# Sums of weight quarters formed one product ahead of their cast, out of place, in two alternating tiles

## The chip, the core and the metric

The kernel runs on one core of a Trainium2 chip. Five engines of the core work side by side, each through its own queue in order: PE (TensorE) multiplies matrices, DVE (VectorE) and ACT (ScalarE) do elementwise work, POOL (GpSimd) does a little of it, and SP (SyncE) issues the loads from memory. They wait for one another only by semaphores. PE appears twice in the profile, as PE (the matmuls) and PEld (the loads of the stationary operand that go ahead of each matmul).

The metric is the device time of one execution in microseconds. Less is better.

## The reference

The program is a two-layer decoder trunk over 512 tokens of width 1024. Each layer is a mixer, a layer norm, a SwiGLU feed-forward block and another layer norm. The change concerns the first half of the feed-forward block, which occurs once in each layer:

```python
D_MODEL, SEQ, DEPTH, D_FF = 1024, 512, 2, 2816

def swiglu(x, w_gate, w_up, w_down):
    return (jax.nn.silu(x @ w_gate) * (x @ w_up)) @ w_down

for layer in range(DEPTH):
    ...
    x = layer_norm(ALPHA * x + y, ln_mix_g[layer], ln_mix_b[layer])
    x = layer_norm(ALPHA * x + swiglu(x, ffn_w_gate[layer], ffn_w_up[layer], ffn_w_down[layer]),
                   ln_ffn_g[layer], ln_ffn_b[layer])
```

All inputs are float32. The kernel keeps that accuracy with three matmuls in a reduced format for each product: every operand is split into a high part `hi` (a cast) and a low part `lo` (the operand minus `hi`), and `hi*hi + hi*lo + lo*hi` is summed.

## The kernel before

**How a feed-forward block runs.** `ffn` (L356) handles the first two of the 22 blocks of 128 hidden features directly, prepares sums of the activations (`sums`, L322), hands the other twenty blocks to `sevens` (L394), and then multiplies by `w_down` in `down` (L276).

**What `sevens` computes.** It takes the twenty blocks as ten pairs. For one pair, `x @ w_gate` and `x @ w_up` together are seen as a product of 2 by 2 block matrices: the tokens in two halves by the inner dimension in two halves, times four weight quarters of 128 partitions by 1024 floats, which the code names `x`, `u`, `y` and `z` (gate upper, up upper, up lower, gate lower). Seven block products in place of eight give the result. Their weight operands, by position 0 to 6, are x, x+u, x+u+y, z, u+y, y, x+u+y+z. So four of the seven weights are sums that DVE must form: those of positions 1, 2, 4 and 6.

**The loop.** `sevens` has 70 steps, seven for each pair. Step i calls `make(i)` (L417), which readies the weight of product i, and `take(i - 4)` (L443), which multiplies with a weight made four steps before (`AHEAD = 4`). All engines follow the program's order in this loop (`manual_schedule`, L502). What each call issues:

- `make(i)` on DVE: where the position has a sum, the sum (L426); then on ACT the cast to `hi` (L98), and on DVE the subtraction that gives `lo` (L104). The cast needs the sum, the subtraction needs the cast, and the next step's sum stands behind this step's subtraction in DVE's queue. The text below writes sum 4, cast 4 and lo 4 for the three operations of position 4, and so on.
- The sums are in place. Position 1 writes x+u into a tile `t` (of tag `lng` for even pairs, `lnb` for odd ones), position 2 adds y to it, position 6 adds z to it; position 4 adds y to the raw tile of u. The two tags are those of the layer norm's scale and offset, whose tiles are not in use here; their next load is issued by `load_ln` (L220) after the loop.
- `take` for position 0 runs 24 matmuls into bank `a` and copies it on ACT to bank `d` (L466); for 1, into `b`, copied to `p5` (L470); for 2, on top of `d`, copied to `e` (L474); for 3, on top of `a`, then Silu on ACT (L478); for 4, on top of `e`, copied to `f` (L482) and added to `p5` on DVE (L483); for 5, on top of `d`, added on DVE (L487), and two multiplications for the first half of the tokens (L460); for 6, on top of `f`, then Silu (L493) and two multiplications for the other half (L460). Product 2 accumulates onto the copy in `d`, so PE cannot start it before the copy of L466 has ended; product 4 needs the copy of L474 in the same way, and product 6 that of L482. In the first products an extra matmul (L454) prepares a bank.

With a lead of four, step i makes the weight at position m while it takes the product at position m+3 (modulo 7). In the queue of ACT the copy of L466 therefore stands behind cast 4 of the next weights.

**Loads and buffers.** Each quarter is one load of 512 KB that SP issues (L409) into a ring of five `raw` tiles; SP waits until the ring's next tile is free. `loads` (L412) fixes the steps: x, u, y, z of pair p are issued at steps 7p-4, 7p-3, 7p-2 and 7p-1. The cast weights go into a ring of five pairs (`pair`, L106; `WP = 5`).

Of the kernel before, what the change touches and what calls it, by code (L numbers as in the profile page):

```python
# [10 lines left out]
F32 = mybir.dt.float32  # L11
# [3 lines left out]
ALU = mybir.AluOpType  # L15
AX = mybir.AxisListType

P = 128
S = 512
NB = S // P  # L20
D = 1024
# [24 lines left out]
def trunk(ctx, tc, a, out):  # L46
# [3 lines left out]
    tt = nc.vector.tensor_tensor  # L50
# [4 lines left out]
    big = ctx.enter_context(tc.tile_pool(name="big", bufs=1))  # L55
# [12 lines left out]
    def nm(s):  # L68
        cnt[0] += 1
        return f"{s}{cnt[0]}"  # L70
# [7 lines left out]
    def temp(tag="tmp", dt=F32):  # L78
        return tmp.tile([P, 512], dt, tag=tag, name=nm(tag))
# [4 lines left out]
    def ps():  # L84
        return psp.tile([P, 512], F32, tag="ps", name=nm("ps"))


    state = {"i": 0, "pool": 0}
# [8 lines left out]
    def split(src, hi, lo, pool=False):  # L97
        nc.scalar.copy(out=hi, in_=src)  # L98
        if pool:
            n = src.shape[1] // 2  # L100
            for c in (slice(0, n), slice(n, 2 * n)):
                nc.gpsimd.tensor_tensor(out=lo[:, c], in0=src[:, c], in1=hi[:, c].bitcast(F32), op=ALU.subtract)
            return
        tt(out=lo, in0=src, in1=hi.bitcast(F32), op=ALU.subtract)  # L104

    def pair(n=D):  # L106
        t = wp.tile([P, 2, D], F32R, tag="w", name=nm("w"))
        return t[:, 0, :n], t[:, 1, :n]
# [247 lines left out]
    def ffn(layer, last, flips):  # L356
# [28 lines left out]
        for f in range(2):  # L385
            for w, bank in first[2 * f:2 * f + 2]:
                gemm_a(bank, w, cols=slice(256, 512))
            finish(f, first[2 * f][1], first[2 * f + 1][1])
        last_sum()
        sevens(sx, hs, hidden_tile)  # L390
        gb = load_ln("ffn", layer)
        return down(hs, [1] * (KF - 5) + [5], gb, last)

    def sevens(sx, hs, hidden_tile):  # L394

        pairs = list(range(DIRECT, KF, 2))
        n = 7 * len(pairs)  # L400
        base = state["i"]
        state["i"] += 4 * len(pairs)
        raw, ws, tiles = {}, {}, {}

        def fetch_quarter(p, name, which):

            raw[p, name] = rawp.tile([P, D], F32, tag="raw", name=nm("raw"))
            i = base + 4 * p + which
            nc.sync.dma_start(out=raw[p, name], in_=a["w"][i // 2, :, (i % 2) * D:(i % 2) * D + D])  # L409


        loads = {}  # L412
        for p in range(len(pairs)):
            for at, args in ((-4, ("x", 0)), (-3, ("u", 1)), (-2, ("y", 2)), (-1, ("z", 3))):
                loads.setdefault(7 * p + at, []).append((p, *args))

        def make(i):  # L417

            p, pos = divmod(i, 7)
            if pos == 1:  # L420
                tag = ("lng", "lnb")[p % 2]
                raw[p, "t"] = big.tile([P, D], F32, tag=tag, name=nm(tag))
            src = raw[p, "xttzuyt"[pos]]
            if pos in (1, 2, 4, 6):
                first = raw[p, "xttzuyt"[0 if pos == 1 else pos]]
                tt(out=src, in0=first, in1=raw[p, {1: "u", 2: "y", 4: "y", 6: "z"}[pos]], op=ALU.add)  # L426
            hi, lo = pair()
            split(src, hi, lo)
            ws[i] = [t.rearrange("p (f k m) -> p f k m", f=2, k=4) for t in (hi, lo)]

        def quarter(k0, t0):
            return [[t[:, k0 + 2 * j:k0 + 2 * j + 2, t0:t0 + 256] for j in range(2)] for t in (xh, xl)]

        def product(bank, w, x, start=True):
            hi, lo = w
            for f in range(2):
                for k in range(4):
                    for m, (l, r) in enumerate(((hi, x[0]), (hi, x[1]), (lo, x[0]))):
                        mm(bank[:, f * 256:f * 256 + 256], lhsT=l[:, f, k, :], rhs=r[k // 2][:, k % 2, :],  # L439
                           start=(start and f == 0 and k == 0 and m == 0), stop=(k == 3 and m == 2),  # L440
                           skip_group_check=True)

        def take(i):  # L443


            p, pos = divmod(i, 7)
            g = tiles
            w = ws.pop(i)

            def primed():  # L450

                bank = ps()
                if p == 0 or (p == 1 and pos == 0):
                    mm(bank, lhsT=w[0][:, 0, 0, :], rhs=xh[:, 0, :], start=True, stop=True)  # L454
                return bank

            def half(n, gate, up):
                for f in range(2):
                    c = slice(f * 256, f * 256 + 256)
                    stt(out=g["h"][f][:, n * 256:n * 256 + 256], in0=gate[:, c], scalar=-1.0, in1=up[:, c],  # L460
                        op0=ALU.mult, op1=ALU.mult)

            if pos == 0:
                g["a"], g["d"] = ps(), primed()
                product(g["a"], w, quarter(0, 0))
                nc.scalar.copy(out=g["d"], in_=g["a"])  # L466
            elif pos == 1:
                g["b"], g["p5"] = ps(), temp("p")
                product(g["b"], w, sx["s1"])
                nc.scalar.copy(out=g["p5"], in_=g["b"])  # L470
            elif pos == 2:
                g["e"] = primed()
                product(g["d"], w, sx["s2"], start=False)
                nc.scalar.copy(out=g["e"], in_=g["d"])  # L474
            elif pos == 3:
                product(g["a"], w, quarter(4, 0), start=False)
                g["g0"] = temp()
                act(out=g["g0"], in_=g["a"], func=AF.Silu)  # L478
            elif pos == 4:
                product(g["e"], w, sx["s3"], start=False)  # L480
                g["f"], g["up1"] = primed(), temp("p")
                nc.scalar.copy(out=g["f"], in_=g["e"])  # L482
                tt(out=g["up1"], in0=g["p5"], in1=g["e"], op=ALU.add)  # L483
            elif pos == 5:
                product(g["d"], w, sx["s4"], start=False)
                up0 = temp("p")
                tt(out=up0, in0=g["p5"], in1=g["d"], op=ALU.add)  # L487
                g["h"] = [hidden_tile(pairs[p] + f) for f in range(2)]
                half(0, g["g0"], up0)
            else:  # L490
                product(g["f"], w, quarter(4, 256), start=False)
                g1 = temp()
                act(out=g1, in_=g["f"], func=AF.Silu)  # L493
                half(1, g1, g["up1"])
                hs.extend(g["h"])

        for at in sorted(loads):
            if at < 0:
                for args in loads[at]:
                    fetch_quarter(*args)  # L500
        E = mybir.EngineType
        with tc.manual_schedule(engines={E.PE, E.Activation, E.DVE, E.Pool, E.SP}):  # L502
            for i in range(n + AHEAD):
                for args in loads.get(i, ()):
                    fetch_quarter(*args)
                if i < n:
                    make(i)
                if i >= AHEAD:
                    take(i - AHEAD)
# [662 lines left out]
```

## Time and profile before

| | |
|---|---|
| median of 3 runs | 1101.81 us (1101.62 to 1101.85) |
| the profiled execution | 1101.23 us |
| its span | 1099.4 us |
| mean granted TensorE clock | 0.993 |
| PE busy, share of the span | 98% |
| DVE busy | 66% |
| ACT busy | 45% |
| first `sevens` on PE | about 200 to 409 us |
| second `sevens` on PE | about 762 to 972 us |

The span is the time from the first to the last recorded work of the profiled execution; the 1.8 us beyond it are the start and the end of the program. An engine's busy share is an average over the whole run, in which stages with different limits follow each other. Matmuls overlap in the pipeline, so PE shows as busy also where it could start its matmuls closer together; the distance between the starts of successive PEld records shows that better. In rows of the timeline the columns are start, duration, engine, line, operation, output and inputs, count, and in brackets the idle time just before and what ended it.

### The profile page before, as it was taken

To read this page: it belongs to the slowest core of one execution; us is meant where nothing else is said; L and a number is where in the kernel's file an instruction comes from. 1 tells how busy PE (TensorE), PEld (TensorE's weight loads), DVE (VectorE), ACT (ScalarE), POOL (GpSimd) and SP (SyncE) were. 2 spreads that over 40 slices of the span, in tenths; PEclk is the share of its full clock that TensorE was granted. 3 is DMA by queue.
4 is the path that set the end of the run, shared out by engine and by line. 5 is a ranking of instruction groups with operands and counts; after the bars stand their busy time and mean duration, and the time that the engine had idled before them with its cause. 6 is when DMAs were issued, how large, how long until landed. Compare 5 with 4: busy or idle time off the path is not lost.

```text
span 1099.4 us, 16995 instructions
## 1 busy us (share of the span) xinstructions
PE 1074.7 (98%) x6936; PEld 966.0 (88%) x6936; DVE 725.7 (66%) x1118; ACT 498.2 (45%) x831; POOL 77.7 (7%) x108
## 2 busy tenths in 40 slices
PE   9999999999999999999999999999999999999997
PEld 7888888899999998888978788888999999988885
DVE  5666449877777783334757885479777777753337
ACT  4544335545545562223466453354544544542221
POOL 0000013000000000000513411030000000000001
PEclk9999999999999999999999999999999999999999
DMA  9522222222323443331341030321332332452202
GB/s 339 194 71 78 77 78 77 75 80 97 131 81 97 144 158 101 96 98 56 96 154 58 1 115 1 102 71 58 106 126 78 107 124 78 124 183 96 96 1 76
DMA packets 31501, 109.38 MB, mean 99 GB/s; under 512 B 3504, under 2 KB 3648, under 8 KB 31424
## 3 DMA queue, kind: packets, MB, share of 16 engines
q1 hardware_dynamic: 31424, 108.31, 29.7%
q8 instruction: 54, 0.88, 0.3%
q14 instruction: 23, 0.19, 0.1%
HBM read 106.20 MB, written 2.10 MB: 99 GB/s over the span
## 4 chain that ended last, share of the span: by engine, by line
PE 57%; DVE 23%; ACT 11%; issue 8%; DMA 1%; POOL 0%; DVEq 0%; SPq 0%; ACTq 0%; POOLq 0%
PE ps L286 27%; PE ps L179 12%; ACT w L98 8%; PE ps L213 6%; DVE w L104 6%; PE ps L439 5%; DVE lng L426 3%; DVE lnb L426 3%; DVE raw L426 2%; DVE wk L460 1%; DVE xn L258 1%; PE ps L898 1%; DVE p L483 1%; DVE p L487 1%; ACT ps L474 1%
## 5 line engine op out<-in xcount | busy, mean ns | idle before, releaser
L286 PE MATMUL ps<-w,hx 128*128 128x512 f32 x1440 | 329.4, 390 | 0.0
L286 PEld LDWEIGHTS ps<-w,hx 128*128 128x128 f32 x1440 | 269.5, 188 | 55.5
L104 DVE TENSOR_TENSOR w<-raw,w 128x1024 fp32r<-128x1024 f32 (+1 forms) x175 | 212.2, 1217 | 74.4 <-ACT w L98 69.7
L439 PE MATMUL ps<-xh,w 128*128 128x256 f32 x1280 | 240.7, 286 | 7.4 <-ACT ps L466 7.4
L98 ACT CAST w<-raw 128x1024 fp32r<-128x1024 f32 (+2 forms) x184 | 189.1, 1036 | 110.8 <-DVE raw L426 73.0
L439 PEld LDWEIGHTS ps<-xh,w 128*128 128x128 f32 x1280 | 203.7, 193 | 11.1 <-ACT ps L466 11.1
L439 PE MATMUL ps<-xl,w 128*128 128x256 f32 x640 | 181.8, 284 | 0.0
L439 PE MATMUL ps<-hx,w 128*128 128x256 f32 x1440 | 179.6, 283 | 0.0
L439 PEld LDWEIGHTS ps<-hx,w 128*128 128x128 f32 x1440 | 176.0, 192 | 0.1
L179 PE MATMUL ps<-xh,w 128*128 128x512 f32 (+1 forms) x608 | 162.0, 350 | 1.1 <-ACT xh L98 1.1
L439 PEld LDWEIGHTS ps<-xl,w 128*128 128x128 f32 x640 | 123.5, 193 | 0.2
L179 PEld LDWEIGHTS ps<-xh,w 128*128 128x128 f32 x608 | 107.1, 190 | 16.7 <-ACT xh L98 1.9
L179 PE MATMUL ps<-xl,w 128*128 128x512 f32 (+1 forms) x304 | 105.4, 347 | 0.0
L104 DVE TENSOR_TENSOR hx<-m,hx 128x512 fp32r<-128x512 f32 x32 | 21.6, 689 | 81.0 <-ACT hx L98 80.9
L179 PEld LDWEIGHTS ps<-xl,w 128*128 128x128 f32 x304 | 58.0, 191 | 6.9 <-DVE xl L104 0.4
L252 POOL TENSOR_TENSOR rs<-ve,neghalf 128x1 f32<-128x1 f32 x16 | 10.5, 655 | 728.6 <-DVE ve L250 695.3
L213 PE MATMUL ps<-w,xh 128*128 128x512 f32 (+1 forms) x192 | 58.0, 383 | 0.0
L104 DVE TENSOR_TENSOR w<-lnb,w 128x1024 fp32r<-128x1024 f32 x30 | 36.7, 1225 | 31.2 <-ACT w L98 31.2
L98 ACT CAST w<-lnb 128x1024 fp32r<-128x1024 f32 x30 | 31.5, 1049 | 57.1 <-DVE lnb L426 57.1
L98 ACT CAST hx<-m 128x512 fp32r<-128x512 f32 x32 | 19.3, 623 | 83.3 <-PE ps L286 83.1
L104 DVE TENSOR_TENSOR w<-lng,w 128x1024 fp32r<-128x1024 f32 x30 | 36.7, 1224 | 29.1 <-ACT w L98 29.0
L98 ACT CAST w<-lng 128x1024 fp32r<-128x1024 f32 x30 | 31.4, 1048 | 51.9 <-DVE lng L426 51.8
(216 smaller groups left out, 1106.7 us busy)
## 6 DMA issues: line engine op xcount, KB each, us to landing
raw<-in_w_dram SPq DMA_DIRECT2D x182, 512.0 KB, 3.9
hx<-in_xT_dram SPq DMA_DIRECT2D x8, 256.0 KB, 6.0
xn<-in_xn_dram SPq DMA_DIRECT2D x4, 512.0 KB, 9.4
out_dram<-xn SPq DMA_DIRECT2D x8, 256.0 KB, 2.0
raw<-in_w_dram SPq DMA_DIRECT2D x4, 256.0 KB, 6.0
lng<-in_ln_mix_g_dram SPq DMA_DIRECT2D x2, 512.0 KB, 7.2
lnb<-in_ln_mix_b_dram SPq DMA_DIRECT2D x2, 512.0 KB, 7.5
lng<-in_ln_ffn_g_dram SPq DMA_DIRECT2D x2, 512.0 KB, 4.8
```

The costliest lines, as they stand in the source:

```text
L98: nc.scalar.copy(out=hi, in_=src)
L104: tt(out=lo, in0=src, in1=hi.bitcast(F32), op=ALU.subtract)
L179: mm(dst[:, cols], lhsT=l[:, k, :], rhs=r[:, k, cols], start=(k == 0 and n == 0), stop=(k == KD - 1 and n == 2))
L213: mm(banks[b][:, :n], lhsT=l[:, k, t], rhs=r[:, c], start=(k == 0 and m == 0), stop=(k == KD - 1 and m == 2))
L258: state["ln"] = stt(out=xn[:, b, hs], in0=r[h], scalar=rs, in1=be[:, hs], op0=ALU.mult, op1=ALU.add)
L286: mm(acc[b][h], lhsT=l[:, bs], rhs=r[:, h * 512:h * 512 + 512], start=(k == 0 and n == 0), stop=(k == nk - 1 and n == 2))
L426: tt(out=src, in0=first, in1=raw[p, {1: "u", 2: "y", 4: "y", 6: "z"}[pos]], op=ALU.add)
L439: mm(bank[:, f * 256:f * 256 + 256], lhsT=l[:, f, k, :], rhs=r[k // 2][:, k % 2, :], start=(start and f == 0 and k == 0 and m == 0), stop= ...
L460: stt(out=g["h"][f][:, n * 256:n * 256 + 256], in0=gate[:, c], scalar=-1.0, in1=up[:, c], op0=ALU.mult, op1=ALU.mult)
L474: nc.scalar.copy(out=g["e"], in_=g["d"])
L483: tt(out=g["up1"], in0=g["p5"], in1=g["e"], op=ALU.add)
L487: tt(out=up0, in0=g["p5"], in1=g["d"], op=ALU.add)
```

## The change

Three things change, all in `sevens`.

1. A new function `total(i)` forms the sum for product i. `make(i)` calls it for i+1, ahead of its own cast and subtraction. So on DVE the sum for the next product comes before the subtraction for this one. Positions without a sum (0, 3, 5) issue nothing there.
2. Of the four sums of a pair, those of positions 1, 2 and 6 are out of place: each takes a fresh tile, with the tags `lng` and `lnb` in turn over the whole loop (`state["sums"]`). Position 2 reads the tile of position 1 and position 6 that of position 2. Position 4 still adds y into the raw tile of u.
3. The loads of x and u are each one step earlier (steps 7p-5 and 7p-4); those of y and z stay.

```diff
+        state["sums"] = 0
...
-            for at, args in ((-4, ("x", 0)), (-3, ("u", 1)), (-2, ("y", 2)), (-1, ("z", 3))):
+            for at, args in ((-5, ("x", 0)), (-4, ("u", 1)), (-2, ("y", 2)), (-1, ("z", 3))):
                 loads.setdefault(7 * p + at, []).append((p, *args))
 
+        def total(i):
+
+            if i >= n:
+                return
+            p, pos = divmod(i, 7)
+            if pos == 4:
+                tt(out=raw[p, 4], in0=raw[p, "u"], in1=raw[p, "y"], op=ALU.add)
+            elif pos in (1, 2, 6):
+                tag = ("lng", "lnb")[state["sums"] % 2]
+                state["sums"] += 1
+                raw[p, pos] = big.tile([P, D], F32, tag=tag, name=nm(tag))
+                r, s = {1: ("x", "u"), 2: (1, "y"), 6: (2, "z")}[pos]
+                tt(out=raw[p, pos], in0=raw[p, r], in1=raw[p, s], op=ALU.add)
+
         def make(i):
 
             p, pos = divmod(i, 7)
-            if pos == 1:
-                tag = ("lng", "lnb")[p % 2]
-                raw[p, "t"] = big.tile([P, D], F32, tag=tag, name=nm(tag))
-            src = raw[p, "xttzuyt"[pos]]
-            if pos in (1, 2, 4, 6):
-                first = raw[p, "xttzuyt"[0 if pos == 1 else pos]]
-                tt(out=src, in0=first, in1=raw[p, {1: "u", 2: "y", 4: "y", 6: "z"}[pos]], op=ALU.add)
+            raw[p, 4] = raw[p, "u"]
+            total(i + 1)
             hi, lo = pair()
-            split(src, hi, lo)
+            split(raw[p, ("x", 1, 2, "z", 4, "y", 6)[pos]], hi, lo)
```

## The prediction

> **What bounds the kernel now.** I read the page's busy times first.
>
> ```profile
> span 1099.4 us, 16995 instructions
> ## 1 busy us (share of the span) xinstructions
> PE 1074.7 (98%) x6936; PEld 966.0 (88%) x6936; DVE 725.7 (66%) x1118; ACT 498.2 (45%) x831; POOL 77.7 (7%) x108
> ```
>
> PE is busy nearly all the time, so the change can gain no more than the pauses of PE that it removes. The waits of PEld, longest total first, begin with one row that lies wholly in `sevens`:
>
> ```profile
> PEld ps L439 <- ACT ps L466: 11.1, 17, 2.7
> ```
>
> Seventeen times a product waited for the copy of L466, 11.1 us in all, 2.7 us at the longest. It is always product 2, which accumulates onto that copy. The timeline of PEld shows one round of the loop:
>
> ```profile
> 291.53 0.19 PEld L439 LDWEIGHTS ps<-xh,w 128*128 128x128 f32 x1 [0.41 <-ACT ps L466]
> ...
> 308.80 2.95 PEld L439 LDWEIGHTS ps<-hx,w 128*128 128x128 f32 x24
> 312.15 0.19 PEld L439 LDWEIGHTS ps<-xh,w 128*128 128x128 f32 x1 [0.40 <-ACT ps L466]
> ```
>
> From the first load of product 2 (291.53) to that of product 1 in the next round (308.80) lie products 2, 3, 4, 5, 6, 0: 6 x 24 = 144 loads in 17.27 us, **0.1199 us each**, or 2.878 us for a product. Product 1 should end at 308.80 + 2.88 = 311.68, but product 2 starts at 312.15. So a pair takes 20.62 us (312.15 - 291.53), of which PE needs 168 x 0.1199 = 20.15; **0.47 us of each pair is lost**. Why the copy is late is seen on DVE and on ACT in the same stretch:
>
> ```profile
> 304.98 1.23 DVE L104 TENSOR_TENSOR w<-lnb,w 128x1024 fp32r<-128x1024 f32 x1 [1.11 <-ACT w L98]
> 306.12 0.68 DVE L487 TENSOR_TENSOR p<-p,ps 128x512 f32<-128x512 f32 x1
> 306.84 0.76 DVE L460 SCALAR_TENSOR_TENSOR wk<-tmp,p 128x256 f32<-128x256 f32 x2
> 307.51 1.22 DVE L104 TENSOR_TENSOR w<-raw,w 128x1024 fp32r<-128x1024 f32 x1
> 308.65 0.75 DVE L460 SCALAR_TENSOR_TENSOR wk<-tmp,p 128x256 f32<-128x256 f32 x2
> 309.32 1.22 DVE L426 TENSOR_TENSOR raw<-raw,raw 128x1024 f32<-128x1024 f32 x1
> 311.65 1.23 DVE L104 TENSOR_TENSOR w<-raw,w 128x1024 fp32r<-128x1024 f32 x1 [1.11 <-ACT w L98]
> ```
>
> ```profile
> 306.29 0.60 ACT L493 ACTIVATE tmp<-ps 128x512 f32<-128x512 f32 x1 [0.40 <-PE ps L439]
> 310.57 1.05 ACT L98 CAST w<-raw 128x1024 fp32r<-128x1024 f32 x1 [3.68 <-DVE raw L426]
> 311.52 0.58 ACT L466 COPY ps<-ps 128x512 f32<-128x512 f32 x1
> 312.04 1.04 ACT L98 CAST w<-raw 128x1024 fp32r<-128x1024 f32 x1
> ```
>
> Product 0 ended when product 1 began, at 308.80, so the copy could have started soon after; Silu at 306.29 shows the lag, since product 6 ended at 308.80 - 2.88 = 305.92: 0.37 us. Instead ACT stood idle 3.68 us for sum 4 (309.32), which on DVE waited behind lo 2, the addition, lo 3 and both pairs of multiplications. Sum, cast, copy: the product starts 0.05 us after the copy. DVE, in turn, idles 1.11 us behind each cast. The pair's period is that alternation, not the work of either engine:
>
> ```profile
> 309.00:330.00 21.00, 20.80 (x173) 20.60 (x172) 16.04 (x20) 10.22 (x13) 0.00 (x0) 1.00 0.30 101
> ```
>
> In these 21 us DVE (third number after the length) is busy 16.04 and ACT 10.22; the granted clock is 1.00.
>
> **The change, steady state.** No operation is added or removed: seven casts, seven subtractions and four sums per pair stay. Out of place costs nothing, by the rows of both forms (minimum, median, maximum in ns):
>
> ```profile
> L426 DVE TENSOR_TENSOR lnb<-lnb,raw x20: 1216/1218/1221, 220.2 to 959.3; 128x1024 f32<-128x1024 f32 x20
> L426 DVE TENSOR_TENSOR lnb<-raw,raw x10: 1217/1218/1220, 216.1 to 943.6; 128x1024 f32<-128x1024 f32 x10
> ```
>
> The new form, `lng` from `lnb` and raw, isn't in the trace; it has three tiles as the second row has, so 0 us, with at most 5 ns either way. A sum now runs beside a cast; the cast at 312.04 ran beside lo 4 and took 1.04, that at 310.57 beside an idle DVE took 1.05, so I take 0 for that too.
>
> Now the order, with times from the start of product 0, products back to back and their results seen 0.37 after their end. DVE: product 5 is seen at 6 x 2.878 + 0.37 = 17.64; addition to 18.3, multiplications to 19.0, then **sum 4 from 19.0 to 20.2**, ahead of lo 3. ACT: product 6 is seen at 20.15 + 0.37 = 20.52; Silu to 21.1; cast 4 has its sum already and runs to 22.1; the copy waits only for product 0 of the next pair, seen at 20.15 + 3.25 = 23.40, and ends at 24.0. Product 2 is due at 20.15 + 5.76 = 25.91. So the copy is 1.9 us early where it was 0.47 late, and PE runs through. What is late next? The copies of L474 and L482 have the same 1.9 us (one product of 2.88 lies between, less 0.37 and 0.58), with casts 6 and 1 done beforehand. The weights are three products ahead: lo 4 ends at 3.3, and its product starts at 11.5. So PE is late next, at 20.15 us a pair.
>
> For the whole stage I use the first and the last of these waits, 208.99 and 394.62 in layer 1, 770.77 and 957.18 in layer 2; each lies nine pairs apart:
>
> ```profile
> 206.12 0.19 PEld L454 LDWEIGHTS ps<-xh,w 128*128 128x128 f32 x1
> 208.99 0.19 PEld L439 LDWEIGHTS ps<-xh,w 128*128 128x128 f32 x1 [2.68 <-ACT ps L466]
> ...
> 770.77 0.19 PEld L439 LDWEIGHTS ps<-xh,w 128*128 128x128 f32 x1 [2.56 <-ACT ps L466]
> ```
>
> ```profile
> 394.62 14.66 PE ps L439 x120
> ...
> 781.17 0.23 PE ps L454
> ...
> 957.18 14.66 PE ps L439 x120
> ```
>
> PE needs 9 x 168 x 0.1199 = 181.33 us and two extra matmuls of L454 at 0.24, 181.8. Layer 1 took 185.63: **gain 3.8**. Layer 2 took 186.41: 4.6, if the clock is full. It was not:
>
> ```profile
> 770.70:774.50 3.80, 3.73 (x18) 3.73 (x19) 3.15 (x3) 1.85 (x4) 0.00 (x0) 0.55 0.45 135
> 774.50:778.30 3.80, 3.80 (x34) 3.80 (x33) 2.46 (x3) 2.20 (x3) 0.00 (x0) 1.00 0.78 254
> ```
>
> After the pause the granted clock was 0.55 for 3.8 us: 19 loads against 33, which is 14 to 15 loads or some 1.6 us lost (before, the alternation was the limit for the next three pairs and swallowed that). So **4.6 without and 3.0 with** that dip.
>
> **The change, start of the stage.** Each first product 2 waited 2.6 us for the same copy. DVE is busy without a break here, with the activation sums:
>
> ```profile
> 204.97 1.22 DVE L104 TENSOR_TENSOR w<-raw,w 128x1024 fp32r<-128x1024 f32 x1
> 206.11 1.22 DVE L426 TENSOR_TENSOR raw<-raw,raw 128x1024 f32<-128x1024 f32 x1
> ```
>
> Lo 3 stands before sum 4; the change swaps them, and the copy comes 1.14 us earlier. In the chain of layer 2 the order is the same:
>
> ```profile
> 765.70 2.27 DVE w L104 x2
> 767.97 1.15 DVE raw L426
> ```
>
> So **2.3 us** for both. Bounds: nothing, if the other additions move ahead too, and all of the pause, 2.87 - 0.24 = 2.6 us per layer, if sum 4 also comes before the activation work that precedes lo 3. I take the swap, as that is the one thing the new order forces.
>
> The clock: of two pauses of almost one length the one in layer 1 left the clock at 1.00, that in layer 2 did not. About 1.5 us of pause remains, so I expect no dip. The Trainium skill (TensorE: Matmul & The Clock Gate, Part 1: The HAM clock gate) has the clock halved after an idle window of about 3.4 us that runs freely; by that rule neither pause should have tripped it, and the trace shows that one of 2.6 us can, so the rule alone doesn't exclude a dip.
>
> **Loads.** The ring keeps its order x, u, y, z. The sums of positions 1 and 2 need u and y one step earlier; u is loaded a step earlier too, y isn't. SP issues y when lo 4 has freed the old u, at 3.3, and sum 2 comes up at about 11.7 behind lo 0 (cast 0 follows the copy of L474, seen 9.0). That leaves 8.4 us for a load of
>
> ```profile
> DMA to landing us min/median/max: 3.5/4.5/6.1
> ```
>
> so 0. The layer norm's scale, which SP loads into `lng`, must now wait for sum 6 of the last pair rather than for lo 6 of the one before, and four weight loads stand behind it on SP:
>
> ```profile
> 379.68 0.33 SPq L223 DMA_DIRECT2D lng<-in_ln_ffn_g_dram  x1
> 382.32 15.97 SPq L94 DMA_DIRECT2D raw<-in_w_dram  x4
> ```
>
> Sum 6 ends at about 4.5 in the last pair; the first of the four would land near 9 and is multiplied after 25.6 (20.15 and one product of `down`): 0.
>
> **Sum**: 3.8 + 4.6 + 2.3 = 10.7 us. The profiled execution becomes 1101.23 - 10.7 = 1090.5 (span 1088.7); the median of the runs lies 0.6 above that execution, so **1091.1 us**. Everything behind `sevens` shifts as it is: the chain's 120 matmuls after the last of these waits end the stage, and no wait at L286, the line of `down`, stands among PEld's.
>
> **Rivals.**
>
> - *The clock dips once as before.* The same work, 1.6 us more: **1092.7**. For it: a pause remains, and the windows move. Against: it is half as long.
> - *The start's pause goes wholly.* Another 1.5 us per layer: **1088**. For it: DVE's order outside the loop is planned anew. Against: the planner put the activation work first before.
> - *Half of the steady gain.* Another copy or the first pairs catch up late, or the start gains nothing: half of 3.8 + 3.0 is 3.4, so 1091.1 + 3.4 = **1094.5**, to about 1097 with the start. Against: 1.9 us of slack at each copy.
> - *Nothing changes.* DVE is the limit and has as much work as before: **1101.8**. For it: DVE is on the chain of waits. Against: 16.04 of 21 us. The Trainium skill (VectorE: DVE Perf Modes, Rules for kernel authors) says to lower the number of operations, since leaving out semaphores gains nothing; by that rule a reordering is worth 0, and the trace disagrees in so far as 1.11 us behind each cast is idle time on another engine.
> - *Slower: y comes late.* Sum 2 now stands ahead of lo 1, so a late y blocks DVE's whole queue. From sum 2 to the end of sum 4 DVE has 6.7 us of work (two sums and two subtractions at 1.14 between starts, two additions and the multiplications at 0.7), and sum 4 must end by 25.91 - 0.58 - 1.0 = 24.3 for product 2 to be on time, so y may land until 17.6, 14.3 us after its issue. From about 15 us on, the change loses (0.6 us in each of 18 pairs eats the gain of 10.7); at 16 us it costs 1.7 a pair, 31 us: 1091.1 + 31 = **1122**. Against: the longest landing is 6.1.
>
> **Chances.** Forecast 0.64, dip 0.16, whole pause 0.05, half 0.05, nothing 0.06, slower 0.04. The range, 1088.0 to 1097.0, takes in the first four and with them the bounds of the start. Faster by over 0.2% (2.2 us, about what a measurement of this kernel can tell from no change): 0.90; within: 0.06; slower: 0.04.
>
> **What would show it.** Right: the waits of PEld for L466 fall from 17 to at most two, at the starts; successive first loads of product 2 stand 20.15 apart; ACT no longer idles for L426 but for PE before L466, L470 and L474; DVE's busy time stays within 1 us of 725.7. Wrong: a wait of PE for L474 or L482, ACT's casts waiting for L426 as before, DVE waiting for a load at L426, or a first wait of 2 us or more with the clock below 1.

## The result and the profile after

The changed kernel takes **1091.57 us** (median of 4 runs, 1090.80 to 1094.18), the kernel before 1101.83 in the same comparison: a ratio of **0.9912, 95% interval 0.9897 to 0.9926**, that is 10 us less. The prediction was 1091.1. The profiled execution is the longest of the four, 1094.18 us, 2.6 us above the median; where it lost time is shown below.

The page's first rows for the changed kernel:

```profile
span 1092.4 us, 16994 instructions
## 1 busy us (share of the span) xinstructions
PE 1071.6 (98%) x6936; PEld 966.6 (88%) x6936; DVE 729.3 (67%) x1118; ACT 498.1 (46%) x831; POOL 78.6 (7%) x108
```

The work is the same; PE's share was 98% before and is 98% now, so that share would have told nothing. The waits of PEld do. Longest total first, they now begin with:

```profile
PEld ps L179 <- DVE xl L271: 5.4, 2, 2.7
```

The 17 waits for the copy into bank `d` (L466 before, L476 now) are gone, all of them, also the two at the starts. In their place stand two waits that were not there before, 2.7 us each, in another part of the feed-forward block. The chain of waits, in order of time (start, length, what), has one long row in each stage:

```profile
223.41 181.43 PE ps L449 x1512
...
783.37 181.43 PE ps L449 x1512
```

Nine pairs are one unbroken piece of 1512 matmuls in 181.43 us, 0.1200 each: before, the chain through the same stretch ran over DVE and ACT. What the stages gained is read from the starts of matmuls on PE: the first of the first product 2 (L449), and the first of `down` (L286).

```profile
208.38 0.28 PE L449 MATMUL ps<-xh,w 128*128 128x256 f32 x1
404.69 0.86 PE L286 MATMUL ps<-w,hx 128*128 128x512 f32 x3
...
768.34 0.28 PE L449 MATMUL ps<-xh,w 128*128 128x256 f32 x1
964.64 0.63 PE L286 MATMUL ps<-w,hx 128*128 128x512 f32 x2
```

In the kernel before, the first products 2 start at 208.99 and 770.77, and `down` at:

```profile
409.12 0.63 PE L286 MATMUL ps<-w,hx 128*128 128x512 f32 x2
...
971.68 0.63 PE L286 MATMUL ps<-w,hx 128*128 128x512 f32 x2
```

So the first stage takes 404.69 - 208.38 = 196.31 us from there, and the second 964.64 - 768.34 = 196.30. Before these were 409.12 - 208.99 = 200.13 and 971.68 - 770.77 = 200.91. The steady part gave **3.8 and 4.6 us**.

One round of the loop on ACT, in the timeline of the changed kernel, with L503 the Silu of product 6 and L476 the copy:

```profile
304.15 0.60 ACT L503 ACTIVATE tmp<-ps 128x512 f32<-128x512 f32 x1 [1.89 <-PE ps L449]
304.64 1.04 ACT L98 CAST w<-raw 128x1024 fp32r<-128x1024 f32 x1
306.97 0.57 ACT L476 COPY ps<-ps 128x512 f32<-128x512 f32 x1 [1.29 <-PE ps L449]
307.45 1.05 ACT L98 CAST w<-raw 128x1024 fp32r<-128x1024 f32 x1
```

and PEld at product 1 of two successive pairs:

```profile
306.65 2.95 PEld L449 LDWEIGHTS ps<-hx,w 128*128 128x128 f32 x24
...
326.81 2.95 PEld L449 LDWEIGHTS ps<-hx,w 128*128 128x128 f32 x24
```

Cast 4 (304.64) follows the Silu without a wait, where it had waited 3.68 us for its sum. ACT idles for PE now, 1.29 us before the copy. The copy ends at 307.54; product 2 is due one product after 306.65, at 309.53. It is early by 2.0 us. A pair takes 326.81 - 306.65 = 20.16 us.

### The profile page after: what moved, and what is told of

Read it like the earlier page. It is cut to its first block, busy times and chain, and to the rows that moved or that the text cites. A ratio compares the mean times of both kernels' runs of the same rounds, so it can differ in the third digit from the quotient of the medians.

```text
span 1092.4 us, 16994 instructions
## 1 busy us (share of the span) xinstructions
PE 1071.6 (98%) x6936; PEld 966.6 (88%) x6936; DVE 729.3 (67%) x1118; ACT 498.1 (46%) x831; POOL 78.6 (7%) x108
## 4 chain that ended last, share of the span: by engine, by line
PE 89%; DVE 7%; issue 1%; ACT 1%; DMA 1%; POOL 0%; DVEq 0%; SPq 0%; ACTq 0%; POOLq 0%
PE ps L449 37%; PE ps L286 27%; PE ps L179 13%; PE ps L213 5%; DVE xn L258 1%; DVE w L104 1%; DVE p L255 1%; PE ps L755 1%; DVE p L234 1%; DVE xl L271 1%; PE ps L908 1%; PE ps L604 1%; PE ps L551 1%; PE ps L591 1%; DVE st L237 1%
## 5 line engine op out<-in xcount | busy, mean ns | idle before, releaser
L286 PE MATMUL ps<-w,hx 128*128 128x512 f32 x1440 | 329.4, 390 | 0.0
L286 PEld LDWEIGHTS ps<-w,hx 128*128 128x128 f32 x1440 | 269.5, 188 | 55.5
L104 DVE TENSOR_TENSOR w<-raw,w 128x1024 fp32r<-128x1024 f32 (+1 forms) x175 | 212.2, 1217 | 65.6 <-ACT w L98 59.7
L449 PE MATMUL ps<-xh,w 128*128 128x256 f32 x1280 | 237.5, 283 | 0.0
L449 PEld LDWEIGHTS ps<-xh,w 128*128 128x128 f32 x1280 | 202.7, 192 | 0.0
L449 PE MATMUL ps<-xl,w 128*128 128x256 f32 x640 | 181.1, 283 | 0.0
L449 PE MATMUL ps<-hx,w 128*128 128x256 f32 x1440 | 179.6, 283 | 0.0
L449 PEld LDWEIGHTS ps<-hx,w 128*128 128x128 f32 x1440 | 175.9, 192 | 0.1
L179 PE MATMUL ps<-xh,w 128*128 128x512 f32 (+1 forms) x608 | 163.5, 353 | 1.4 <-ACT xh L98 1.4
L179 PEld LDWEIGHTS ps<-xh,w 128*128 128x128 f32 x608 | 108.2, 193 | 17.0 <-ACT xh L98 2.0
L449 PEld LDWEIGHTS ps<-xl,w 128*128 128x128 f32 x640 | 122.8, 192 | 0.3
L179 PE MATMUL ps<-xl,w 128*128 128x512 f32 (+1 forms) x304 | 106.3, 350 | 5.2 <-DVE xl L271 5.0
L104 DVE TENSOR_TENSOR hx<-m,hx 128x512 fp32r<-128x512 f32 x32 | 21.6, 689 | 81.0 <-ACT hx L98 81.0
L179 PEld LDWEIGHTS ps<-xl,w 128*128 128x128 f32 x304 | 58.7, 193 | 12.6 <-DVE xl L271 5.4
L104 DVE TENSOR_TENSOR hx<-wk,hx 128x512 fp32r<-128x512 f32 x28 | 19.3, 690 | 51.8 <-ACT hx L98 51.8
L104 DVE TENSOR_TENSOR w<-lnb,w 128x1024 fp32r<-128x1024 f32 x30 | 36.8, 1225 | 21.1 <-ACT w L98 21.1
L104 DVE TENSOR_TENSOR w<-lng,w 128x1024 fp32r<-128x1024 f32 x30 | 36.8, 1225 | 20.4 <-ACT w L98 20.3
L98 ACT CAST hx<-wk 128x512 fp32r<-128x512 f32 x28 | 17.4, 622 | 64.0 <-PE ps L286 61.4
```

What stands on the lines that cost most here:

```text
L179: mm(dst[:, cols], lhsT=l[:, k, :], rhs=r[:, k, cols], start=(k == 0 and n == 0), stop=(k == KD - 1 and n == 2))
L286: mm(acc[b][h], lhsT=l[:, bs], rhs=r[:, h * 512:h * 512 + 512], start=(k == 0 and n == 0), stop=(k == nk - 1 and n == 2))
```

## The new pause at the start

Why do the two waits at L179 exist? Below is DVE in the timeline of the changed kernel. L430 at 186.50 is sum 1, L104 is lo 0, L430 at 188.77 is sum 2, and L271 makes the low part of the last block's activations, which the matmuls of L179 need:

```profile
185.30 1.28 DVE L271 TENSOR_TENSOR xl<-ps,xh 128x512 fp32r<-128x512 f32 x2
186.50 1.22 DVE L430 TENSOR_TENSOR lng<-raw,raw 128x1024 f32<-128x1024 f32 x1
187.63 1.22 DVE L104 TENSOR_TENSOR w<-raw,w 128x1024 fp32r<-128x1024 f32 x1
188.77 1.22 DVE L430 TENSOR_TENSOR lnb<-lng,raw 128x1024 f32<-128x1024 f32 x1
189.90 1.28 DVE L271 TENSOR_TENSOR xl<-ps,xh 128x512 fp32r<-128x512 f32 x2
```

and PEld behind it:

```profile
190.64 0.19 PEld L179 LDWEIGHTS ps<-xl,w 128*128 128x128 f32 x1 [2.71 <-DVE xl L271]
```

In the kernel before, only sum 1 stood there:

```profile
186.67 1.21 DVE L426 TENSOR_TENSOR lng<-raw,raw 128x1024 f32<-128x1024 f32 x1
187.80 0.68 DVE L271 TENSOR_TENSOR xl<-ps,xh 128x512 fp32r<-128x512 f32 x1
```

Outside the loop the planner decides where the loop's operations fall among the others. It put sum 1, lo 0 and sum 2 in a row ahead of the subtraction. In return lo 0 and the two subtractions of the third block (L271) left the middle of the layer norm's last block, which ends sooner by that, and a pause of PE ahead of that block's flips (the transposes of L266) is gone. It stood there before:

```profile
186.15 0.42 PEld L266 LDWEIGHTS ps<-pack,xn 128*128 128x128 f32 x4 [1.25 <-issue]
```

And sum 4 came out ahead of most of the activation sums, so that the copy waits for PE only:

```profile
205.47 0.57 ACT L476 COPY ps<-ps 128x512 f32<-128x512 f32 x1 [0.46 <-PE ps L449]
```

In each stage, two pauses (about 1.3 and 2.6 us) were traded for one of 2.7. From the flips of the layer norm's third block to product 2, by matmul starts on PE, layer 1 takes 29.08 us (179.30 to 208.38), before 30.28 (178.71 to 208.99): 1.2 us gained. In layer 2 it is 30.41 (737.93 to 768.34) against 30.15 (740.62 to 770.77), 0.3 us lost. There the clock fell behind the pause; the chain has 95 matmuls behind each of the two:

```profile
190.64 11.67 PE ps L179 x95
...
749.27 13.00 PE ps L179 x95
```

```profile
749.20:752.00 2.80, 2.73 (x13) 2.73 (x14) 2.06 (x5) 1.96 (x4) 0.00 (x0) 0.50 0.35 140
```

The granted clock was 0.50 in 2.8 us, and 1.3 us went there. The terms of this execution add up to 3.82 + 4.61 + 1.20 - 0.26 = 9.37 us. Of these 2.33 were lost outside the stages: 0.59 before the flips of the first, where the granted clock was 0.83 between 5 and 15 us (1.00 before), and 1.74 in the second mixer (404.69 to 737.93 is 333.24 us, before 409.12 to 740.62, 331.50), where it was 0.50 from 650 to 655. That leaves 7.04 us, and the two profiled executions differ by 7.05. Another profiled execution of the same kernel, among the experiments, took 1090.73 us: its two stages are as long (452.23 us together from the flips to `down`, here 452.10), and the difference lies ahead of the first (1.5 us) and in the second mixer (2.1 us).

## The experiments

Two theories were tried first. **A, the cycle:** a pair's period before was a closed round of DVE and ACT taking turns, 20.62 us long, and shortening it anywhere by more than 0.47 us frees PE. **B, the one wait:** only sum 4 counts, since only its copy made PE wait. The first four kernels ran together, then the next four, and the last three side by side.

**Sum 4 alone ahead**, on the kernel before:

```diff
-            if pos in (1, 2, 4, 6):
+            if pos in (1, 2, 6):
                 first = raw[p, "xttzuyt"[0 if pos == 1 else pos]]
                 tt(out=src, in0=first, in1=raw[p, {1: "u", 2: "y", 4: "y", 6: "z"}[pos]], op=ALU.add)
+            if pos == 3:
+                d, s = {4: ("u", "y"), 6: ("t", "z")}[4]
+                tt(out=raw[p, d], in0=raw[p, d], in1=raw[p, s], op=ALU.add)
```

> The kernel before with one edit: sum 4 alone is formed one step early, ahead of lo 3, still in place; the other sums, the tiles and the loads as before. Theory A (the period of 20.62 us is a cycle of DVE and ACT taking turns, and shortening it anywhere by more than 0.47 us makes PE the limit) and theory B (only the wait of the copy at L466 for sum 4 counts) both expect the whole steady gain, 8.4 us, a pair at 20.15 us and no wait for that copy after the start. Sums 1 and 2 are not ahead, so the pause of 2.7 us before L179 that the changed kernel has should be absent, and the pause before the first product 2 should be 1.1 us shorter than before in each layer. Time 1091 us, about that of the changed kernel. Rival C (all four sums must be ahead): above 1097.

Measured: 1089.83 us, ratio 0.9900 (0.9884 to 0.9917). PEld's longest wait, with L469 the copy:

```profile
PEld ps L442 <- ACT ps L469: 3.0, 2, 1.5
```

Two waits, both at the starts and 1.1 us shorter than those of before (1.55 and 1.42 against 2.68 and 2.56), no wait at L179 for the subtraction, and in both stages 1512 matmuls in 181.43 us again, 20.16 us a pair: as expected on each point. One sum moved by one step gives what the whole change gives, or a little more.

**Sum 6 alone ahead**, the same edit with 6 for 4 and `pos == 5` for `pos == 3`:

> The kernel before with one edit: sum 6 alone is formed one step early, ahead of lo 5, still in place; sum 4 stays in its old place in front of the copy at L466. Theory A (a cycle): any one sum taken out of the cycle shortens it by 1.1 us, more than the 0.47 that are missing, so a pair still takes 20.15 us and PE waits for the copy only at the start, 2.7 us as before: 1093.5 us. Theory B (one wait): sum 4 stands where it stood, a pair keeps 20.6 us and PE waits at least 14 times: 1101 us or more.

Measured: 1094.03 us, 0.9939 (0.9924 to 0.9954).

```profile
PEld ps L442 <- ACT ps L469: 5.2, 2, 2.7
```

PE waits for the copy at the two starts only. Yet sum 4 stands where it stood, directly ahead of the cast that holds up the copy, as one round of the loop shows (cast 4 and the copy on ACT, product 1 on PEld):

```profile
308.19 1.05 ACT L98 CAST w<-raw 128x1024 fp32r<-128x1024 f32 x1 [2.77 <-DVE raw L426]
309.14 0.58 ACT L469 COPY ps<-ps 128x512 f32<-128x512 f32 x1
```

```profile
307.32 2.95 PEld L442 LDWEIGHTS ps<-hx,w 128*128 128x128 f32 x24
...
327.48 2.95 PEld L442 LDWEIGHTS ps<-hx,w 128*128 128x128 f32 x24
```

Cast 4 still waits 2.77 us for its sum. But the copy ends at 309.72, and product 2 is due at 307.32 + 2.88 = 310.20: it is 0.5 us early where it was 0.47 late, and a pair takes 20.16 us. **Theory B falls.** The copy was late because the whole round was 0.47 us too long; it was enough to cut it at sum 6, far from the wait.

**All but sum 4 ahead**, on the changed kernel:

```diff
-            total(i + 1)
+            if pos == 4:
+                total(i)
+            if pos != 3:
+                total(i + 1)
```

> The changed kernel with sum 4 put back behind lo 3 and in front of its own cast; sums 1, 2 and 6 stay ahead. Theory A: a pair takes 20.15 us, since three sums are out of the cycle. Theory B: about 20.6 us and waits of PE for the copy again. At the start the pause of 2.7 us before L179 stays, as sums 1 and 2 are ahead, and a pause of about 1.2 us before the first product 2 comes back: 1094 us by theory A, 1102 by theory B.

Measured: 1095.57 us, 0.9951 (0.9934 to 0.9967); profiled execution 1098.06.

```profile
PEld ps L179 <- DVE xl L271: 5.4, 2, 2.7
PEld ps L452 <- ACT ps L479: 2.9, 2, 1.7
```

Theory A again: nothing in the pairs (181.43 us for nine), and both kinds of pause at the starts, 2.7 and 1.3 to 1.7 us. The time lies 1.6 us above the 1094 expected; in the profiled execution the clock fell behind both pauses of 2.7 us.

**No sum ahead**, on the changed kernel (`total(i)` for `total(i + 1)`), which leaves the alternating tiles and the earlier loads:

> The changed kernel with each sum in its old place, in front of its own cast; what is left of the change are the alternating tiles out of place and the loads of x and u one step earlier. If those two cost and bring nothing, as the prediction has it: 1101.8 us within 1.5, a pair at 20.62 us, 17 waits for the copy, 11 us in all. If the earlier loads or the tiles bring part of the gain: below 1099.

Measured: 1100.93 us, 1.0001 (0.9990 to 1.0012).

```profile
PEld ps L449 <- ACT ps L476: 11.2, 17, 2.7
```

The same 17 waits as before: with the sums in their old places, those two parts cost nothing and bring nothing. By the code, the fresh tiles are what allows sum 2 to go ahead of lo 1, since in place it would overwrite x+u before lo 1 has read it. Sum 4 alone, or sum 6 alone, needs none.

**One more sum in the kernel before**, in the cycle:

```diff
                 tt(out=src, in0=first, in1=raw[p, {1: "u", 2: "y", 4: "y", 6: "z"}[pos]], op=ALU.add)
+                if pos == 1 and p:
+                    tt(out=src, in0=first, in1=raw[p, "u"], op=ALU.add)
```

> The kernel before with sum 1 formed twice in a row from the second pair on (the same tile, the same values): one more operation of 1.14 us in each of 18 pairs. Theory A (the pair's period is the cycle of DVE and ACT): the operation lies on the cycle, so it costs its whole length, 18 x 1.14 = 20.5 us, and the pair takes 21.8 us: 1122 us. Rival (DVE has 4.6 us of idle time in a pair, so one more operation fits): no change, 1101.

Measured (two runs): 1124.21 us, 1.0206 (1.0185 to 1.0227), 22.4 us more than the kernel before beside it. PEld at product 2 of two successive pairs:

```profile
252.92 0.19 PEld L441 LDWEIGHTS ps<-xh,w 128*128 128x128 f32 x1 [1.68 <-ACT ps L468]
274.81 0.19 PEld L441 LDWEIGHTS ps<-xh,w 128*128 128x128 f32 x1 [1.69 <-ACT ps L468]
```

21.89 us a pair, 1.27 more than 20.62. That is more than the 1.14 expected: the second addition writes the same tile and starts 1.26 us after the first (259.96 and 261.22), where successive operations on different tiles start 1.14 apart in this trace (258.82 and 259.96). DVE had idle time for the operation, but the cycle had not.

**Three more sums in the changed kernel:**

```diff
-                tt(out=raw[p, pos], in0=raw[p, r], in1=raw[p, s], op=ALU.add)
+                for _ in range(4 if pos == 1 and p else 1):
+                    tt(out=raw[p, pos], in0=raw[p, r], in1=raw[p, s], op=ALU.add)
```

> The changed kernel with sum 1 formed four times in a row from the second pair on (the same tile, the same values): three more operations of 1.14 us in each of 18 pairs, so DVE has 16.0 + 3.4 = 19.4 us of work in a pair of 20.15. Theory A: the alternation is broken and PE is the limit, so nothing changes: 1091.6 us within 2, a pair at 20.15 us, no wait of PE for the copy. Rival (the changed kernel's period still rests on DVE's chain): up to 18 x 3.4 = 61 us more.

Measured (two runs): 1090.88 us, 0.9904 (0.9884 to 0.9923), not told apart from the changed kernel's 0.9912. The busy times of 21 us in the middle of the stage (PE, PEld, DVE, ACT, POOL after the length):

```profile
309.00:330.00 21.00, 21.00 (x178) 21.00 (x177) 19.72 (x22) 10.48 (x13) 0.00 (x0) 1.00 0.35 107
```

DVE is busy 94% of the time, and PE does not wait. The same kind of operation cost 1.27 us when it lay on the cycle and nothing, three times over, when it didn't.

**The first pair's sums 1 and 2 put back**, in the changed kernel:

```diff
-            total(i + 1)
+            if i in (1, 2):
+                total(i)
+            if i + 1 not in (1, 2):
+                total(i + 1)
```

> The changed kernel with sums 1 and 2 of the first pair alone in their old places, in front of their own casts. If the pause of 2.7 us before L179 comes from these two standing ahead of the subtraction at L271 in DVE's queue, it is gone in both layers and the old order of the start is back: a pause of 1.5 us before the first product 2, 1090 us, as with sum 4 alone ahead. If that pause has another cause, it stays and so does the time, 1091.6.

Measured: 1090.46 us, 0.9907 (0.9889 to 0.9925).

```profile
PEld ps L452 <- ACT ps L479: 3.0, 2, 1.5
```

The waits at L179 are gone from the list and the shortened pause before product 2 is back, so the two sums made the new pause. The time is not told apart from the changed kernel's: its runs spread from 1087.90 to 1092.86.

**Sum 4 alone, two steps ahead**, on the kernel before: as in the first experiment with `pos == 2` for `pos == 3`.

> The kernel before with one edit: sum 4 alone is formed two steps early, in place, between sum 2 and lo 2. Steady state as with sum 4 one step early: 20.15 us a pair. At the start sum 4 then also precedes the last activation sums on DVE, so the pause before the first product 2, 1.5 us with one step, should fall to 0.2 or less in each layer, with no pause of 2.7 us before L179: 2.6 to 2.8 us less than with one step, 1087 us. If the lo 2 that it pushes back becomes the wait instead, the pause stays at about 1 us and the time at 1089.

Measured: 1088.29 us, 0.9882 (0.9868 to 0.9897). Of the waits for the copy none is left; one wait of 0.22 us, for another copy, stands in the first stage:

```profile
212.84 2.94 PEld L442 LDWEIGHTS ps<-hx,w 128*128 128x128 f32 x24 [0.22 <-ACT ps L477]
```

The pauses went as expected; the median is 1.5 us below that of one step, measured in the first group, and not 2.6 to 2.8.

**The three side by side**, in one comparison on one chip: first the changed kernel,

> The changed kernel again, beside the next two on one chip. From the pauses in the traces: 5.4 us before L179 at the two starts, none in the pairs. 1091.5 us, ratio 0.990 to 0.992; 2 us more than the next, 3 to 4 us more than the one after it.

then sum 4 one step ahead,

> Sum 4 alone one step early, again. Pauses: 3.0 us before the first products 2 and 2.5 us at the flips of the layer norm's last block, none in the pairs: 1089.5 us, ratio 0.988 to 0.990.

then two steps ahead:

> Sum 4 alone two steps early, again. Pauses: 2.5 us at the flips, 0.2 us in the first stage: 2.5 us less than with one step if the stages alone decide, 1087 us, ratio 0.986 to 0.988; if the run before last (1088.3 against 1089.8) had it right, 1.5 us less.

| kernel | median, us | lowest to highest | ratio to before, 95% interval |
|---|---|---|---|
| changed kernel | 1092.10 | 1090.73 to 1092.68 | 0.9918 (0.9903 to 0.9933) |
| sum 4 one step ahead | 1090.55 | 1089.33 to 1091.93 | 0.9906 (0.9891 to 0.9921) |
| sum 4 two steps ahead | 1088.94 | 1088.27 to 1089.76 | 0.9889 (0.9873 to 0.9906) |

The order is as expected and the steps are 1.6 us each. Both ratios with sum 4 alone lie a little above the range expected, so these two kernels gained less than was expected of them. No run of the third kernel was as slow as any run of the changed kernel. The intervals of the ratios overlap, so a difference between the second kernel and either of its neighbours is likely rather than shown. The smallest edit, one sum two steps early and in place, gives the most.

Why 1.6 us from one step to two, where the pauses promise 2.5? The record answers in part. From the flips of the third block to the first matmul of `down`, the two stages together took 450.96 and 450.98 us in the two profiled executions with one step, 448.41 and 448.40 in those with two: 2.6 us less, as expected. Outside the stages, where the kernels have the same code, the executions with two steps are 1.9 and 2.2 us longer, at lower mean granted clocks (0.995 and 0.994 against 0.997 in both). Whether that is chance or follows from the change stays open.

## Why the prediction was right, and which step was not

- **What bounds the kernel.** Right: 0.47 us of each pair were lost to the alternation of DVE and ACT, not to the work of either. The two experiments with added sums show both halves of that sentence.
- **The price of the tiles and the loads**, nothing: right, by the kernel with no sum ahead.
- **Steady gain**, 3.8 and 4.6 us: 3.8 and 4.6 measured. PE's 0.1199 us per load held, at 0.1200. The copy was forecast 1.9 us early and is 2.0 us early.
- **The start**, 2.3 us: **the mechanism failed**. The step said: "I take the swap, as that is the one thing the new order forces", and expected a pause of about 1.5 us to remain before product 2. The new order forces more. Sums 1 and 2 also move ahead, and lo 0 behind sum 1, into the last block of the layer norm, where the planner set them before L271. The pause before product 2 went wholly, one of 2.7 us came before L179, and one of about 1.3 us went. The kernel whose start does follow the swap is the one with sum 4 alone ahead: there the pauses are 1.5 us, as worked out.
- **The size of the start was luck.** In each layer pauses of 3.9 us (1.3 and 2.6) became one of 2.7; the forecast had 3.9 become 2.8 (1.3 and 1.5). So layer 1 gained 1.2 us and layer 2 would have gained 1.1 without the dip of the clock, close to the 1.14 forecast for each, by another way. Without that dip the two stages give 9.4 + 1.3 = 10.7 us, the forecast's sum. That the median came within 0.5 us of the forecast rests on this coincidence too.
- **The clock.** Forecast without a dip, because the remaining pause would be short. It was not short, and in each of the two profiled executions of the changed kernel the clock fell at one of the two starts, behind the new pause (1.3 us in the one shown, forecast at 1.6). The rival "the clock dips once as before" is what these executions did, though its pause was another. The sign named for being wrong, a first wait of 2 us or more with the clock below 1, appeared, but at L179.
- **The rival "the start's pause goes wholly"** had its condition right, that DVE's order outside the loop is planned anew: the pause before product 2 did go. Its price, another 1.5 us per layer, didn't come, since the new pause took it. Sum 4 alone, two steps ahead, is the kernel in which it came (1088.29 and 1088.94).
- **DVE's busy time** was to stay within 1 us of 725.7; the page has 729.3. That sign failed. The durations of all groups together rose by 1.1 us only (770.6 to 771.7), so the rest is less overlap between successive operations; why there is less is not shown.
- **The other rivals.** No wait for a load appears at the sums, so y was not late, and `down` starts without a wait. DVE as the limit is ruled out by the kernel with three more sums. The rival "half of the steady gain" took half of 3.8 + 3.0, the sum with the dip, from a forecast made without it; half of 8.4 would be 4.2 and the time 1095.3.

## What to carry to other kernels

When two engines hand work to each other several times in a loop, add up the round trip and compare it with the busy engine's period. If it is longer by a little, moving one operation from between two hand-overs to beside one can remove the loss, and the wait that the profile names need not be the place to cut: here sum 4 alone and sum 6 alone each did it. Move as little as possible: what moves ahead in the first round also moves ahead of the work before the loop.

## What the runs showed of the hardware

At the starts of the stages, a pause of PE of 2.5 to 2.7 us was followed by a dip of the granted clock in about half of the cases. Of 16 such pauses in eight profiled executions (two of the changed kernel) 9 were followed by some 3 us near half clock and 7 were not. Before product 2 it was all four in layer 2 and none of four in layer 1; before L179 it was five of eight, and the same place in the changed kernel went either way. The Trainium skill (TensorE: Matmul & The Clock Gate, Part 1: The HAM clock gate) speaks of at least one idle window of about 3.4 us; these shorter pauses contradict that as a lower bound.

At these places no dip followed a pause of 1.7 us or less. That is no safe limit: in the second mixer of the changed kernel the clock fell to 0.51 behind a stretch with several waits in a row, of which the longest was 1.75 us (the granted clock is the number after POOL's count):

```profile
566.21 0.29 PEld L726 LDWEIGHTS ps<-tmp,wk 16*128 16x128 f32 x2 [1.75 <-issue]
```

```profile
568.00:570.00 2.00, 2.00 (x5) 1.49 (x5) 1.39 (x2) 1.79 (x3) 0.00 (x0) 0.51 0.63 162
```

Such dips, in the second mixer and at the start of the program too, are likely what spreads the runs of one kernel by 1 to 5 us; that was seen in the profiled executions only.
